# A denser pace of expert gathers in the middle groups, and expert choice that may run on into the dense stage

## The chip, the cores and the metric

The kernel runs on one core of one Trainium2 chip. The metric is the device time of one execution in microseconds (us). The engines are named as in the profile: PE (TensorE matmul), PEld (its weight loads), DVE (VectorE), ACT (ScalarE), POOL (GpSimd) and SP (SyncE, which here only issues DMAs).

## The reference, cut to what matters

One layer over 1152 rows of width 1024, taken as nine tiles of 128 rows (tiles 0 to 7 and a sample tile, here row 8). First a mixer (a gated convolution and an RWKV-7 branch with many projections), then PEER, a retrieval over 16384 single-neuron experts:

```python
q = (xt @ wq).reshape(PEER_BLOCK, PEER_HEADS, 2, PEER_HALF)
s = jnp.einsum('thpd,hpnd->thpn', q, keys).astype(jnp.float32)
s_top, i_top = lax.top_k(s, PEER_TOPK)
...
sc, pos = lax.top_k(cand, PEER_TOPK)
eidx = jnp.take_along_axis(cidx, pos, axis=-1)
gate = jax.nn.softmax(sc, axis=-1)
u = jnp.take(U, eidx, axis=0)
act = jax.nn.gelu(jnp.einsum('thkd,td->thk', u, xt).astype(jnp.float32))
coef = (gate * act).astype(xt.dtype)
return jnp.einsum('thk,thkd->td', coef, jnp.take(V, eidx, axis=0))
```

Each token has 8 heads of 16 experts, so a tile of 128 tokens needs 128 gathers from `U` and 128 from `V`, each of 128 rows of 4 KB.

## The kernel before, in words

The mixer runs over three groups of three tiles: `base(0)`, `base(1)`, `base(2)`. Below, these are group 0 and the two middle groups, 1 and 2. Each streams all the weights through `split_w`: a 256 KB load on SP, a copy to `wh` on ACT (line 246) and the subtraction that gives `wl` on POOL (line 248). PE then multiplies. A group ends with the scores of the expert keys and their top 16 on DVE (`top`).

PEER is done in two ways. Rows 3 to 6 (`DENSE`) are done densely: `dense()` multiplies these 512 tokens with all the experts. Its first half, `gates_of`, builds coefficient tables out of one-hot tiles (`o1`, `o2`), and `hidden_ahead` runs beside it. Its second half, here the main loop, runs over 32 groups of four blocks of 128 experts; per group it has 72 matmuls into `ph` and 96 into `po`, and DVE makes 8 `vl`, 8 `acc`, 4 `ge`, 4 `ph` and 3 `ul` tiles. Rows 0, 1, 2, 7 and 8 are done sparsely: `sparse_u` issues 128 gathers from `peer_u` on POOL (line 1026), each followed by a dot product on DVE into `hu` (called a u step here); `sparse_v` issues 128 gathers from `peer_v` (line 1073), each followed by four matmuls into `sv` on PE in the trace (a v step). All gathers share six `gt` buffers. That makes 1280 steps, 640 of each kind. `side()` runs the v steps of one row beside the u steps of the next, two by two, or one kind alone when the other has no row ready.

Two tables of numbers set the order. `run()` lays out the main work and counts its PE time in `P.ns`; it puts in a sparse step whenever `state[1]` falls behind `P.ns`, and then moves `state[1]` on by `pace()`. In the middle groups that is `PACE_B`, its first number while both kinds run and its second while one runs alone. In the dense stage it is the time that is left over the steps that are left, so that the steps end 40 us (`EARLY`) before the counted end. `route()` is the expert choice of one row; it is cut into pieces of `SPREAD` units by `yield`, and `routes()` takes the rows one after the other, with at most three sparse rows between their choice and the end of their `sparse_v` (`live`). `weave` puts the pieces of `routes()` between the pieces of a group; what is left of them when the group is at its end follows in one block. A scheduler then orders the instructions of each engine once more by its own estimate of time, so that the order on an engine isn't quite the order of the code; on the chip each engine keeps to its order.

Of the kernel before, what the change touches and what calls it, by code (L numbers as in the profile page):

```python
# [27 lines left out]
DENSE = [3, 4, 5, 6]  # L28
# [2 lines left out]
NPT = 8  # L31
NSL = 27
LAT = 350
SPREAD = 16
PACE_B = (1400, 1900)
EARLY = 40e3
NGT, NGD = 6, 0
AWAY = [4, 5, 6, 7]
# [58 lines left out]
def body(ctx, tc, A):  # L97
# [13 lines left out]
    def T(pool, shape, dt=F32, tag=None, bufs=None):  # L111
        _c[0] += 1
        kw = {}
        if tag is not None:
            kw["tag"] = tag
        if bufs is not None:
            kw["bufs"] = bufs
        return pool.tile(shape, dt, name=f"{tag or 'c'}_{_c[0]}", **kw)
# [31 lines left out]
    P = Tensor()  # L150

    class Vector:


        last = None
# [26 lines left out]
    def rk_ps(shape=(128, 512)):  # L182
        return T(spare[0], list(shape), F32, spare[1], spare[2])
# [116 lines left out]
    def slot():  # L300
        return T(bp, [128, 392], F32, "sl", NSL)
# [15 lines left out]
    def base(g):  # L317
# [6 lines left out]
        last = g == len(GROUPS) - 1  # L324
# [546 lines left out]
        def top(hp, q):  # L871
            kt_ = T(bp, [128, 128], F32, "keys", 2)
            nc.sync.dma_start(kt_, A["keys"][hp])
            ps = rk_ps()
            for j in range(len(tiles)):
                P.matmul(ps[:, j * 128:(j + 1) * 128], q[:, j * 128:(j + 1) * 128], kt_, start=True, stop=True)
            sc = slot()
            S.activation(sc[:, :n], ps[:, :n], AF.Copy)
            for j in range(len(tiles)):
                s_ = sc[:, j * 128:(j + 1) * 128]  # L880
                va, vb = vals[j][:, hp, 0:8], vals[j][:, hp, 8:16]
                V.max(va, s_)
                V.max_index(idxs[j][:, hp, 0:8], va, s_)
                V.match_replace(out=s_, in_to_replace=va, in_values=s_, imm_value=NEG)
                V.max(vb, s_)
                V.max_index(idxs[j][:, hp, 8:16], vb, s_)

        for hp in range(16):
# [8 lines left out]
            q = slot()  # L897
            S.activation(q[:, :n], ps[:, :n], AF.Copy)
            yield
        def end():  # L900
            top(15, q)
            for j in range(len(tiles)):
                route_q.append((row0 + j, vals[j], idxs[j]))

        if last:
            end()
        else:
            rest.append(end)

    def route(row, vals, idxs):  # L910
# [13 lines left out]
        for h in range(8):  # L924
            V.max(sc[:, h, 0:8], cand[:, h])
            V.max_index(pos[:, h, 0:8], sc[:, h, 0:8], cand[:, h])
            V.match_replace(out=cand[:, h], in_to_replace=sc[:, h, 0:8], in_values=cand[:, h], imm_value=NEG)
            V.max(sc[:, h, 8:16], cand[:, h])
            V.max_index(pos[:, h, 8:16], sc[:, h, 8:16], cand[:, h])
            yield 3 if row == 0 else SPREAD  # L930
        posf = T(sp, [128, 128], BF, "posf", 1)
        V.tensor_copy(posf, pos.rearrange("p h k -> p (h k)"))
        ix = T(sp, [128, 16, 16], BF, "ixf", 1)
# [12 lines left out]
        for q in range(4):  # L946
            ks, hs = slice(32 * q, 32 * q + 32), slice(2 * q, 2 * q + 2)
            pf = posf[:, ks]
            ge = T(sp, [128, 32, 16], BF, "lk", 2)
            V.tensor_tensor(ge, pf[:, :, None].to_broadcast([128, 32, 16]),  # L950
                            stc[:, None, :].to_broadcast([128, 32, 16]), op=OP.is_ge)
            pr = T(sp, [128, 512], F32, "cand", 1).rearrange("p (a b) -> p a b", b=16)
            V.tensor_tensor(pr.rearrange("p (h k) r -> p h k r", h=2), ge.rearrange("p (h k) r -> p h k r", h=2),
                            d1[:, hs, None, :].to_broadcast([128, 2, 16, 16]), op=OP.mult)
            V.tensor_reduce(i12[:, 2, ks], pr, axis=AX.X, op=OP.add)
            yield 3 if row == 0 else SPREAD
        V.tensor_copy(ints[:, 0], i12[:, 2])
        V.tensor_scalar(ints[:, 1], ints[:, 0], 6, None, op0=OP.arith_shift_right)
        V.tensor_copy(i12[:, 0], ints[:, 1])
# [1 line left out]
        for q in range(4):  # L961
            ks, hs = slice(32 * q, 32 * q + 32), slice(2 * q, 2 * q + 2)
            r2 = T(sp, [128, 32], BF, "r2", 1)
            V.tensor_tensor(r2, posf[:, ks], i12[:, 2, ks], op=OP.subtract)
            ge = T(sp, [128, 32, 16], BF, "lk", 2)
            V.tensor_tensor(ge, r2[:, :, None].to_broadcast([128, 32, 16]),
                            iot[:, None, :].to_broadcast([128, 32, 16]), op=OP.is_equal)
            pr = T(sp, [128, 32, 16], BF, "lk", 2)
            V.tensor_tensor(pr.rearrange("p (h k) r -> p h k r", h=2), ge.rearrange("p (h k) r -> p h k r", h=2),
                            i4[:, hs, 1, None, :].to_broadcast([128, 2, 16, 16]), op=OP.mult)  # L970
            V.tensor_reduce(i12[:, 1, ks], pr, axis=AX.X, op=OP.add)
            yield 3 if row == 0 else SPREAD
        yield 6 if row == 0 else 2 * SPREAD
        gate = T(sp, [128, 8, 16], F32, "gate_d", 1) if row in DENSE else T(sp, [128, 8, 16], F32, "gate", 3)
        V.tensor_tensor(gate, sc, sc[:, :, 0:1].to_broadcast([128, 8, 16]), op=OP.subtract)
        S.activation(gate, gate, AF.Exp)
# [4 lines left out]
        if row not in DENSE:  # L981
            V.scalar_tensor_tensor(i12[:, 2], i12[:, 0], 128.0, i12[:, 1], op0=OP.mult, op1=OP.add)
            ei = T(sp, [128, 128], I32, "ei", 3)
            V.tensor_copy(ei, i12[:, 2])
        yield 6 if row == 0 else SPREAD
        ps = rk_ps()
        if row in DENSE:
            for q, src in enumerate((i12[:, 0], i12[:, 1], gate.rearrange("p h k -> p (h k)"))):
# [5 lines left out]
        else:  # L994
# [1 line left out]
            et = T(sp, [128, 128], I32, "et", 3)  # L996
            V.tensor_copy(et, ps[:, 0:128])
            sparse_q.append((row, ei, et, gate))
        yield 6 if row == 0 else 2 * SPREAD

    more = [None, 0]

# [265 lines left out]
    steps, until = [0], [None]  # L1268
    n_steps = 256 * (9 - len(DENSE))

    def pace(alone):
        if until[0] is None:
            return PACE_B[alone]
        return max(until[0] - P.ns, 0) / (n_steps - steps[0] + 8)
# [17 lines left out]
    def routes():  # L1292
        while rest:
            yield 0.01
        while route_q:
            while route_q[0][0] not in DENSE and live[0] == 3:
                at = P.ns
                yield 0.5
                if P.ns == at:
                    return  # L1300
            live[0] += route_q[0][0] not in DENSE
            yield from route(*route_q.pop(0))


    live, lists = [0], set()
    sparse_q, sparse_v_q, route_q = [], [], []
    run(base(0))
    for g in range(1, len(GROUPS)):
        run(weave([routes()], base(g)))
# [3 lines left out]
    spare[:] = [pd, "ph", 2]  # L1313
    P.in_order = False
    run(weave([routes()], dense()))
    for _ in itertools.chain(state[0] or (), side()):
        pass
    assert not route_q and steps[0] == n_steps


# [70 lines left out]
```

## Time and profile before

| | us |
|---|---|
| median of 3 runs (4288.79 to 4294.24) | 4293.37 |
| the profiled execution, its own time | 4300.95 |
| its span from first to last instruction | 4299.2 |
| group 0 (0 to 529.5) | 529.5 |
| group 1 (529.5 to 1222.2) | 692.7 |
| group 2 (1222.2 to 2009.9) | 787.7 |
| from the last matmul of group 2 to the first of the dense stage | 55.2 |
| coefficient tables (2065.1 to 2545) | 479.9 |
| main loop (2545 to 4036.3) | 1491.3 |
| from the last `po` matmul to the end | 262.9 |

A table of stretches gives the busy time of each engine in each of these seven stretches, with the granted clock of TensorE as a share of full speed and the mean share of the 16 DMA engines. A row of a group of instructions gives the busy time of the group, the mean time of one, the idle time of its engine just before them and what ended that. Lists of waits give the total, the number and the longest.

### The profile page before, as it was taken

What the parts mean: (1) busy time and instruction counts of PE and PEld (TensorE: products, weight loads), DVE (VectorE), ACT (ScalarE), POOL (GpSimd) and SP (SyncE); (2) the same over time, 40 slices, a digit from 0 to 9 for tenths busy, and PEclk for the clock granted to TensorE, in tenths of its full rate; (3) what the DMA queues carried; (4) which work ended last, traced back from release to release, by engine and by line L of the source; (5) the groups of instructions that cost most, each with busy time, mean ns of one, the idle gap of its engine ahead of it and who ended that gap; (6) DMA issues with size and microseconds to landing.
All of it is one profiled execution on the core that took longest, in us unless ns stands there. A gap on an engine that the chain in (4) does not pass through costs nothing. (4 is left out here: it accounts for less than half of the span.)

```text
span 4299.2 us, 56205 instructions
## 1 busy us (share of the span) xinstructions
PE 3731.6 (87%) x18870; PEld 2680.9 (62%) x18870; DVE 2776.8 (65%) x6970; ACT 1473.3 (34%) x3379; POOL 2216.9 (52%) x2009
## 2 busy tenths in 40 slices
PE   7999977887888888785699969999999999999765
PEld 6777865666656555563477747766667766676411
DVE  3654698968797865868767756666666666656400
ACT  4454523443423333231467742222222222222100
POOL 4434455647777554765365643354434344434454
PEclk9999987979989989987799989999999999999888
DMA  3223445557877665786598787899988899987788
GB/s 96 72 65 101 152 141 180 184 162 239 290 262 255 203 209 195 255 281 228 177 355 325 293 314 272 302 332 336 317 286 287 303 320 330 332 293 269 273 305 321
DMA packets 415584, 1065.20 MB, mean 248 GB/s; under 512 B 44992, under 2 KB 124992, under 8 KB 413248
## 3 DMA queue, kind: packets, MB, share of 16 engines
q0 software_dynamic: 184464, 671.55, 45.4%
q1 hardware_dynamic: 182880, 271.03, 19.5%
q10 hardware_dynamic: 47952, 119.03, 7.5%
q8 instruction: 150, 2.46, 0.2%
q14 instruction: 138, 1.13, 0.1%
HBM read 1000.55 MB, written 61.28 MB: 247 GB/s over the span
## 5 line engine op out<-in xcount | busy, mean ns | idle before, releaser
L1026 POOL DMA_INDIRECT gt<-peer_u,ei x640 | 758.0, 1184 | 1149.5 <-PE sv L142 706.7
L159 DVE SCALAR_TENSOR_TENSOR gt<-gt,xn 128x1024 f32<-128x1024 f32 x640 | 855.0, 1346 | 199.0 <-DMA gt<-peer_u,ei 176.7
L142 PE MATMUL mm<-xT,wh 128*128 128x384 f32 (+1 forms) x2880 | 890.6, 367 | 17.8 <-ACT wh L246 15.8
L1073 POOL DMA_INDIRECT gt<-peer_v,et x640 | 677.4, 1059 | 384.0 <-issue 118.9
L248 POOL TENSOR_TENSOR wl<-raw,wh 128x512 fp32r<-128x512 f32 x432 | 577.6, 1345 | 368.7 <-ACT wh L246 320.3
L142 PE MATMUL sv<-gt,c 128*32 128x512 f32 x2560 | 653.7, 636 | 108.1 <-DMA gt<-peer_v,et 107.4
L142 PE MATMUL po<-vh,ph 128*128 128x512 f32 x2048 | 656.8, 394 | 0.0
L142 PEld LDWEIGHTS mm<-xT,wh 128*128 128x128 f32 x2880 | 556.4, 198 | 96.6 <-issue 54.8
L142 PE MATMUL mm<-xT,wl 128*128 128x384 f32 (+1 forms) x1440 | 509.8, 354 | 56.2 <-POOL wl L248 56.2
L142 PEld LDWEIGHTS po<-vh,ph 128*128 128x128 f32 x2048 | 382.3, 188 | 131.9 <-issue 45.3
L142 PEld LDWEIGHTS sv<-gt,c 128*32 128x32 f32 x2560 | 127.8, 114 | 478.6 <-issue 314.7
L142 PE MATMUL ph<-xth,uh 128*128 128x512 f32 x1024 | 408.4, 399 | 18.3 <-ACT ge L1166 17.4
L246 ACT ACTIVATE wh<-raw 128x512 fp32r<-128x512 f32 x432 | 270.2, 629 | 419.6 <-PE mm L142 217.9
L142 PE MATMUL ph<-xth,ul 128*128 128x512 f32 x1024 | 407.0, 397 | 0.0
L142 PE MATMUL ph<-xtl,uh 128*128 128x512 f32 x1024 | 404.0, 395 | 0.0
L142 PE MATMUL po<-vl,ph 128*128 128x512 f32 x1024 | 402.9, 394 | 0.0
L142 PEld LDWEIGHTS mm<-xT,wl 128*128 128x128 f32 x1440 | 286.6, 199 | 78.2 <-POOL wl L248 70.2
L1193 ACT ACTIVATE vh<-vr 128x512 fp32r<-128x512 f32 x256 | 159.7, 627 | 418.9 <-PE po L142 363.4
L1166 ACT ACTIVATE ge<-ph 128x512 f32<-128x512 f32 x128 | 76.7, 599 | 567.5 <-PE ph L142 567.3
L159 DVE TENSOR_TENSOR ge<-ge,cc 128x512 f32<-128x512 f32 x128 | 88.2, 692 | 257.8 <-ACT ge L1166 244.4
L142 PEld LDWEIGHTS ph<-xth,uh 128*128 128x128 f32 x1024 | 193.4, 189 | 77.4 <-ACT ge L1166 18.9
L159 DVE TENSOR_TENSOR acc<-po,acc 128x512 f32<-128x512 f32 x256 | 168.9, 686 | 106.8 <-PE po L142 106.7
(243 smaller groups left out, 5543.0 us busy)
## 6 DMA issues: line engine op xcount, KB each, us to landing
ur<-u_t SPq DMA_DIRECT2D x128, 512.0 KB, 5.4
vr<-peer_v ACTq DMA_DIRECT2D x256, 256.0 KB, 6.1
raw<-w_in SPq DMA_DIRECT2D x240, 256.0 KB, 3.0
c<-ct ACTq DMA_DIRECT2D x16, 2048.0 KB, 10.1
cc<-c SPq DMA_DIRECT2D x32, 1024.0 KB, 17.3
raw<-peer_wq SPq DMA_DIRECT2D x96, 256.0 KB, 3.9
raw<-w_pab SPq DMA_DIRECT2D x48, 256.0 KB, 3.0
raw<-w_o SPq DMA_DIRECT2D x48, 256.0 KB, 3.4
```

The source lines that it names most:

```text
L142: ins = nc.tensor.matmul(out, lhsT, rhs, **kw)
L159: self.last = getattr(nc.vector, name)(*a, **kw)
L246: S.activation(h, part, AF.Copy)
L248: G.tensor_tensor(lo, part, f32(h), op=OP.subtract)
L1026: G.indirect_dma_start(out=ug, out_offset=None, in_=A["peer_u"], in_offset=bass.IndirectOffsetOnAxis(ap=ei[:, k:k + 1], axis=0))
L1073: G.indirect_dma_start(out=vg, out_offset=None, in_=A["peer_v"], in_offset=bass.IndirectOffsetOnAxis(ap=et[:, t:t + 1], axis=0))
L1166: S.activation(g, ps, AF.Gelu_apprx_tanh)
L1193: S.activation(h, raw, AF.Copy)
```

## The change

`PACE_B` goes from (1400, 1900) to (900, 1500). `SPREAD` becomes a pair: 16 as before in the groups, 8 once the dense stage has begun. `routes()` may stop in the middle of a row at the end of a group and go on from there in the next stage; what is under way is kept in `under`. The last group's rows are chosen in the order 7, 6, 8 in place of 6, 7, 8.

```diff
-SPREAD = 16
-PACE_B = (1400, 1900)
+SPREAD = (16, 8)
+PACE_B = (900, 1500)
...
+            if last:
+                route_q.sort(key=lambda q: [7, 6, 8].index(q[0]) if q[0] > 5 else -1)
...
-            yield 3 if row == 0 else SPREAD
+            yield 3 if row == 0 else SPREAD[until[0] is not None]
...
     def routes():
         while rest:
             yield 0.01
-        while route_q:
-            while route_q[0][0] not in DENSE and live[0] == 3:
-                at = P.ns
-                yield 0.5
-                if P.ns == at:
-                    return
-            live[0] += route_q[0][0] not in DENSE
-            yield from route(*route_q.pop(0))
-
-
-    live, lists = [0], set()
+        while route_q or under[0]:
+            if under[0] is None:
+                ns = 0.5
+                if route_q[0][0] in DENSE or live[0] < 3:
+                    live[0] += route_q[0][0] not in DENSE
+                    under[0] = route(*route_q.pop(0))
+            if under[0]:
+                ns = next(under[0], None)
+                if ns is None:
+                    under[0] = None
+                    continue
+            at = P.ns
+            yield ns
+            if P.ns == at:
+
+                return
+
+
+    live, lists, under = [0], set(), [None]
```

What this does to the order of the engines is shown at three places. In the rows, a name is a tile with a number of its own.

PE at the end of the program before, from the last rows of the dense main loop (`po`) on; `sv_28786` is row 7's v sum, `sv_32947` row 8's:

```order
L142 MATMUL po_35481<-vl_35540,ph_35314 128x512
L142 MATMUL po_35481<-vh_35538,ph_35316 128x512
L142 MATMUL sv_28786<-gt_32720,c_108 32x512
L142 MATMUL sv_28786<-gt_32714,c_108 32x512
L142 MATMUL sv_28786<-gt_32720,c_108 32x512
L142 MATMUL sv_28786<-gt_32714,c_108 32x512
```

PE in the changed program where the last `sv` rows stand (`sv_32381` is again row 8's):

```order
L142 MATMUL sv_32381<-gt_35045,c_108 32x512
L142 MATMUL sv_32381<-gt_35001,c_108 32x512
L142 MATMUL po_35105<-vh_35127,ph_34550 128x512
L142 MATMUL po_35106<-vh_35127,ph_34548 128x512
L142 MATMUL po_35106<-vl_35129,ph_34548 128x512
L142 MATMUL po_35106<-vh_35127,ph_34550 128x512
```

Before, 272 `sv` rows (136 v steps, two rows each) stand behind the last `po`; now none does, and some 240 rows of `ph` and `po` follow the last `sv`.

PE before, from the end of group 2 to the first matmul of the dense stage (`po` from `xr`); `rk` from `i` and `gate_d` are the transposes at the end of the expert choice of rows 5, 6 and 7:

```order
L142 MATMUL rk_18573<-keys_18571,sl_18549 128x128 x3
L147 MATMUL rk_18603<-c_74,i_3971_17463 128x128 x2
L147 MATMUL rk_18603<-c_74,gate_d_18596 128x128
L142 MATMUL sv_17632<-gt_18410,c_108 32x512
L142 MATMUL sv_17632<-gt_18404,c_108 32x512
L142 MATMUL sv_17632<-gt_18410,c_108 32x512
L142 MATMUL sv_17632<-gt_18404,c_108 32x512
L147 MATMUL rk_18729<-c_74,i_4214_18668 128x128 x2
L147 MATMUL rk_18729<-c_74,gate_d_18722 128x128
L147 MATMUL rk_18858<-c_74,i_4246_18794 128x128
L147 MATMUL po_18877<-c_74,xr_18875 128x128 x4
```

PE in the changed program at the same place:

```order
L142 MATMUL mm_19291<-xT_17974,wh_19300 128x384
L142 MATMUL rk_19373<-keys_19371,sl_19351 128x128 x3
L142 MATMUL sv_14321<-gt_17763,c_108 32x512
L142 MATMUL sv_14321<-gt_17756,c_108 32x512
L142 MATMUL sv_14321<-gt_17763,c_108 32x512
L142 MATMUL sv_14321<-gt_17756,c_108 32x512
L142 MATMUL sv_14321<-gt_17820,c_108 32x512
L142 MATMUL sv_14321<-gt_17814,c_108 32x512
L142 MATMUL sv_14321<-gt_17820,c_108 32x512
L142 MATMUL sv_14321<-gt_17814,c_108 32x512
L147 MATMUL po_19418<-c_74,xr_19416 128x128 x4
```

The transposes of the expert choice no longer stand ahead of the first dense matmul; on DVE their work is spread between the one-hot tiles of the first three quarters of `gates_of`.

DVE in the main loop before (`gt` with `hu` is the dot product of a u step):

```order
L159 TENSOR_TENSOR acc_23806<-po_27709,acc_23806 128x512
L159 TENSOR_TENSOR vl_27933<-vr_27929,vh_27931 128x512
L159 TENSOR_TENSOR acc_23806<-po_27710,acc_23806 128x512
L159 TENSOR_TENSOR acc_23806<-po_27711,acc_23806 128x512
L159 TENSOR_TENSOR acc_23806<-po_27712,acc_23806 128x512
L159 TENSOR_TENSOR vl_27951<-vr_27947,vh_27949 128x512
L159 SCALAR_TENSOR_TENSOR gt_26474,hu_24593<-gt_26474,xn_24588 128x1024
L159 SCALAR_TENSOR_TENSOR gt_26477,hu_24593<-gt_26477,xn_24588 128x1024
```

DVE in the changed program's main loop, in the fifth of its 32 groups:

```order
L159 SCALAR_TENSOR_TENSOR gt_25539,hu_24299<-gt_25539,xn_24294 128x1024
L159 TENSOR_TENSOR ul_26564<-ur_26560,uh_26562 128x1024
L159 SCALAR_TENSOR_TENSOR gt_25542,hu_24299<-gt_25542,xn_24294 128x1024
L159 SCALAR_TENSOR_TENSOR gt_25545,hu_24299<-gt_25545,xn_24294 128x1024
L159 SCALAR_TENSOR_TENSOR gt_25548,hu_24299<-gt_25548,xn_24294 128x1024
L159 TENSOR_TENSOR ge_26420<-ge_26420,cc_26274 128x512
L159 TENSOR_TENSOR ul_26712<-ur_26708,uh_26710 128x1024
```

In eight of the 32 groups the dots are now about 16 per group with no `sv` beside them, where it was 6 to 12 with 12 to 24 `sv` rows in every group; the last eight groups have no dots at all.

Counted by stage in the two programs, this is where the steps stand:

| steps | before: u, v | changed: u, v |
|---|---|---|
| gathers on POOL by the end of group 1 | 150, 24 | 174, 46 |
| gathers on POOL ahead of the first one-hot tile | 277, 150 | 344, 218 |
| v on PE: ahead of the dense stage / tables / main loop / behind it | 146 / 78 / 280 / 136 | 214 / 150 / 276 / 0 |
| dots on DVE: ahead of the dense stage / tables / main loop and behind it | 275 / 80 / 285 | 342 / 42 / 256 |

## Rows read from the trace of the kernel before

**Rows 1.** The page's first part: busy time, share of the span and instructions
```profile
PE 3731.6 (87%) x18870; PEld 2680.9 (62%) x18870; DVE 2776.8 (65%) x6970; ACT 1473.3 (34%) x3379; POOL 2216.9 (52%) x2009
```

**Rows 2.** Seven stretches: start:end, length, then the columns that the first line names
```profile
core 0: us, PE busy (x) PEld busy (x) DVE busy (x) ACT busy (x) POOL busy (x), PEclk, DMA share, GB/s
0.00:529.50 529.50, 476.25 (x2978) 412.09 (x2979) 277.55 (x963) 261.98 (x690) 229.93 (x225) 0.94 0.32 98
529.50:1222.20 692.70, 550.06 (x3070) 443.91 (x3069) 582.18 (x1626) 256.77 (x679) 442.09 (x366) 0.87 0.63 203
1222.20:2009.90 787.70, 642.91 (x3642) 457.40 (x3639) 580.70 (x1743) 252.97 (x658) 504.44 (x430) 0.90 0.72 239
2009.90:2065.10 55.20, 1.58 (x4) 0.66 (x4) 54.56 (x254) 5.49 (x14) 1.73 (x2) 0.50 0.15 54
2065.10:2545.00 479.90, 421.18 (x2256) 307.19 (x2256) 325.14 (x888) 315.96 (x737) 275.53 (x279) 0.94 0.84 310
2545.00:4036.30 1491.30, 1487.52 (x6381) 1029.63 (x6383) 932.82 (x1454) 372.08 (x576) 625.20 (x564) 1.00 0.88 304
4036.30:4299.20 262.90, 152.11 (x545) 30.00 (x545) 23.81 (x50) 7.99 (x25) 138.02 (x144) 0.84 0.87 304
```

**Rows 3.** Tile sv: PE instructions, count, ns min/median/max, first and last start
```profile
L142 PE MATMUL sv<-gt,c x2560: 589/592/1064, 1125.1 to 4282.1; 128*32 128x512 f32 x197
L147 PE MATMUL sv<-c,hu x5: 270/273/476, 1120.2 to 4066.2; 128*128 128x128 f32 x5
```

**Rows 4.** Groups behind the last po, 4036.3:4299.2: count | busy, mean ns | idle before
```profile
L142 PE MATMUL sv<-gt,c 128*32 128x512 f32 x544 | 151.7, 694 | 87.2 <-DMA gt<-peer_v,et 86.6 <-DVE c L159 0.6
L1073 POOL DMA_INDIRECT gt<-peer_v,et x132 | 125.6, 951 | 98.6 <-PE sv L142 68.7 <-issue 25.6 <-DVE gt L159 2.5
```

**Rows 5.** Waits of PE between group 2 and the dense stage (2009.9 to 2065.1)
```profile
PE rk L147 <- DVE i L159: 37.4, 2, 24.3
PE rk L147 <- DVE sc L159: 26.5, 1, 26.5
```

**Rows 6.** Groups of instructions in group 1 (529.5 to 1222.2)
```profile
L159 DVE SCALAR_TENSOR_TENSOR gt<-gt,xn 128x1024 f32<-128x1024 f32 x148 | 217.4, 1488 | 8.0 <-DMA gt<-peer_u,ei 5.7 <-PE mm L142 1.2 <-PE sv L142 0.7
L248 POOL TENSOR_TENSOR wl<-raw,wh 128x512 fp32r<-128x512 f32 x142 | 192.4, 1363 | 86.1 <-ACT wh L246 76.5 <-issue 8.1
L1026 POOL DMA_INDIRECT gt<-peer_u,ei x150 | 188.2, 1255 | 117.3 <-DVE gt L159 66.6 <-issue 14.2 <-PE mm L142 5.1
```

**Rows 7.** Groups of instructions in group 2 (1222.2 to 2009.9)
```profile
L159 DVE SCALAR_TENSOR_TENSOR gt<-gt,xn 128x1024 f32<-128x1024 f32 x127 | 195.1, 1544 | 66.3 <-DMA gt<-peer_u,ei 64.2 <-PE mm L142 1.3 <-issue 0.4
L248 POOL TENSOR_TENSOR wl<-raw,wh 128x512 fp32r<-128x512 f32 x144 | 191.5, 1341 | 54.3 <-ACT wh L246 45.5 <-issue 6.2 <-PE sv L147 1.0
L1026 POOL DMA_INDIRECT gt<-peer_u,ei x127 | 144.4, 1137 | 133.9 <-PE sv L142 56.2 <-DVE gt L159 39.1 <-issue 13.7
L1073 POOL DMA_INDIRECT gt<-peer_v,et x127 | 141.3, 1113 | 91.9 <-DVE gt L159 36.2 <-PE sv L142 21.5 <-issue 16.6
```

**Rows 8.** Groups of instructions in the main loop (2545 to 4036.3)
```profile
L142 PE MATMUL sv<-gt,c 128*32 128x512 f32 x1122 | 268.1, 598 | 0.0
L159 DVE SCALAR_TENSOR_TENSOR gt<-gt,xn 128x1024 f32<-128x1024 f32 x283 | 343.3, 1220 | 72.9 <-DMA gt<-peer_u,ei 67.2 <-issue 3.1 <-DMA gt<-peer_v,et 1.9
L159 DVE TENSOR_TENSOR vl<-vr,vh 128x512 fp32r<-128x512 f32 x256 | 174.7, 687 | 50.1 <-ACT vh L1193 50.1
L159 DVE TENSOR_TENSOR acc<-po,acc 128x512 f32<-128x512 f32 x255 | 168.2, 686 | 106.8 <-PE po L142 106.7
L159 DVE TENSOR_TENSOR ul<-ur,uh 128x1024 fp32r<-128x1024 f32 x89 | 109.0, 1225 | 14.6 <-ACT uh L1155 14.0 <-PE po L142 0.3 <-DMA cc<-c 0.3
L159 DVE TENSOR_TENSOR ge<-ge,cc 128x512 f32<-128x512 f32 x128 | 88.2, 692 | 257.8 <-ACT ge L1166 244.4 <-DMA cc<-c 13.3
L159 DVE TENSOR_TENSOR ph<-ge,ph 128x512 fp32r<-128x512 f32 x128 | 87.9, 689 | 49.7 <-ACT ph L1236 48.4 <-issue 0.8 <-PE po L142 0.3
```

**Rows 9.** Groups of instructions of the coefficient tables (2065.1 to 2545)
```profile
L142 PE MATMUL sv<-gt,c 128*32 128x512 f32 x312 | 80.6, 639 | 14.5 <-DMA gt<-peer_v,et 14.5
```

More of the change, by code (lines that the diff above doesn't have):

```diff
@@ L955, in route @@
             V.tensor_reduce(i12[:, 2, ks], pr, axis=AX.X, op=OP.add)
-            yield 3 if row == 0 else SPREAD
+            yield 3 if row == 0 else SPREAD[until[0] is not None]
         V.tensor_copy(ints[:, 0], i12[:, 2])
@@ L971, in route @@
             V.tensor_reduce(i12[:, 1, ks], pr, axis=AX.X, op=OP.add)
-            yield 3 if row == 0 else SPREAD
-        yield 6 if row == 0 else 2 * SPREAD
+            yield 3 if row == 0 else SPREAD[until[0] is not None]
+        yield 6 if row == 0 else 2 * SPREAD[until[0] is not None]
         gate = T(sp, [128, 8, 16], F32, "gate_d", 1) if row in DENSE else T(sp, [128, 8, 16], F32, "gate", 3)
@@ L984, in route @@
             V.tensor_copy(ei, i12[:, 2])
-        yield 6 if row == 0 else SPREAD
+        yield 6 if row == 0 else SPREAD[until[0] is not None]
         ps = rk_ps()
@@ L998, in route @@
             sparse_q.append((row, ei, et, gate))
-        yield 6 if row == 0 else 2 * SPREAD
+        yield 6 if row == 0 else 2 * SPREAD[until[0] is not None]
     more = [None, 0]
@@ L1317, in body @@
         pass
-    assert not route_q and steps[0] == n_steps
+    assert not route_q and not under[0] and steps[0] == n_steps
 def kernel(**inputs):
```

## The prediction

> **What bounds the kernel now.** The page first: PE is busy 87% of the span, DVE 65%, POOL 52% [rows 1]. That average mixes stages with different limits, so the table of stretches comes next [rows 2]. In the main loop PE is busy 1487.5 of 1491.3 us at full clock: PE bounds it, and whatever is put on PE there costs its own time. In the coefficient tables PE is busy 421 of 480. In groups 1 and 2 no engine is full (PE 79% and 82%, DVE 84% and 74%, POOL 64% and 64%, DMA 63% and 72%); they wait on one another in small pieces, and the only measure of what a gather costs there is how much longer they take than group 0, which has no gathers. Two stretches are nearly pure loss. In the 55.2 us ahead of the dense stage PE works 1.6 us and DVE 54.6: PE waits there for the expert choice, 37.4 and 26.5 us by the list of waits [rows 5]. Behind the last `po` lie 262.9 us in which only gathers are left: row 8's v sum begins at 4066.2 and ends at 4282.1 [rows 3], and PE waits 86.6 us for gathers to land [rows 4]. The changed order bears on just these two.
>
> **The change part by part.** The sum is made against the profiled execution (4300.95 us, 7.6 over the median of 4293.37).
>
> *The end.* In the changed order no v step stands behind the last `po`, and the last `sv` has about 240 rows of PE work behind it. So the 262.9 us [rows 2] become the finish of the dense rows alone. Before, from the last `sv` (4282.1) to the end of the span (4299.2) it is 17 us for one row [rows 3]; four rows share most of that, and I take 20, with 16 and 35 as ends. **-243 us** (-228 to -247).
>
> *The gap.* The expert choice of rows 5 (its rest), 6, 7 no longer stands on PE between group 2 and the dense stage. What stays is the top 16 of the last key scores and the first `xr`. I take 10 us of the 55.2 as left: **-45** (-25 to -55). The DVE work itself isn't gone; it goes beside the tables (below).
>
> *Groups 1 and 2.* By the counts of the two programs, 427 gathers stand ahead of the first one-hot tile before and 562 now: 135 more, 67 u and 68 v. Group 1 is 163.2 us longer than group 0 with 174 gathers, group 2 258.2 us longer with 254 [rows 2, 6, 7] (group 1's 24 v gathers are from the counts). That is 0.94 and 1.02 us per gather, expert choice and the sample tile included, and the price doesn't rise much with density. From below, a gather could cost only what PE must do for the v sums: 268.1 us for 1122 matmuls, four to a step, is 0.96 us per v [rows 8], so 68 x 0.96 = 65 us with the u steps hidden. From above, the price is that of a stretch with nothing but gathers: 4066.2 to 4282.1 over 128 is 1.69 us [rows 3], so 228 us. The nearest rows are those of the same groups, so I take 1.05: **+142**.
>
> A dot takes 1488 and 1544 ns in groups 1 and 2, where POOL also splits weights, and 1220 in the main loop, where it doesn't [rows 6 to 8]. The 67 dots that move therefore grow by about 0.3 us, 20 us of DVE, which the price per gather already holds. The Trainium skill (SBUF — State Buffer, section "SBUF: two separate sides") speaks against this move: DVE and GpSimd share a pair of ports, and a DVE operation with two SBUF inputs and a GpSimd operation that reads SBUF shut each other out for a whole instruction. The rows agree that there is such a cost, but at a quarter of a whole split of 1.34 us per dot.
>
> *The coefficient tables.* PE gets 150 v steps there in place of 78. Before, 312 matmuls cost 80.6 us there, 1.03 us a step [rows 9]: 72 x 1.03 = 74. Some could fill the 59 us in which PE idles (then about +45); on the other side DVE gets the expert choice of three rows and a rest, some 75 us going by the 54.6 us of the gap [rows 2] for two rows and a rest, and loses 38 dots at 1.22 = 46. DVE is busy 325 of 480 us there, so it has the room, but its order is fixed and PE may wait behind a piece of it. **+75** (+45 to +105).
>
> *The main loop.* Four v steps fewer, 4 x 0.96: -4. But the steps no longer come in pairs all along: for eight of the 32 groups only u steps are there. A group's PE work without v steps is (1491.3 - 268.1) us over the 6381 - 1122 = 5259 other matmuls of the loop, 0.233 each [rows 2, 8], times 168 = 39.1 us. Its DVE work is 8 x 0.687 + 8 x 0.686 + 3 x 1.225 + 4 x 0.692 + 4 x 0.689 = 20.2, and with 16 dots at 1.22 another 19.5: 39.7 us [rows 8]. So in these eight groups DVE draws level with PE. Before, DVE waited 72.9 us over 283 dots for gathers to land, 0.26 each [rows 8], which PE's length hid; here nothing hides it: 16 x 0.26 = 4.2, so 43.9 - 39.1 = 4.8 us a group, 38 in all. If DVE runs ahead of that in the groups on either side it is less. I take +30 (0 to +70). Behind the u steps the loop is bound by PE as before, and six groups with 18 to 34 v steps each have 54 to 72 us for them, over 2 us a gather against 1.69. **+26** (-4 to +66).
>
> *SPREAD, PACE_B and the order 7, 6, 8* have no cost of their own; they act through the counts. Row 6's list must be there for the fourth table; it ends in the second quarter of the counted time of that stage, ahead of need.
>
> *Sum:* -243 - 45 + 142 + 75 + 26 = **-45 us**, 4256 on the profiled scale, 4293.4 - 45 = **4248** on that of the median.
>
> **The rivals.**
> A, *the u steps are free in the middle groups.* PE idles 142 and 145 us in groups 1 and 2 [rows 2], and if the moved u steps fill only that, the term is 65 to 90 in place of 142, and the time 4293 - 97 to 4293 - 122: about **4185**. Against it: group 1 has 150 u and 24 v gathers and yet costs 0.94 a gather.
> B, *POOL's queue is what breaks, and the kernel is slower.* In group 2 a gather holds POOL for (144.4 + 141.3)/254 = 1.12 us and waits in front of it for (133.9 + 91.9)/254 = 0.89 us for one of six buffers [rows 7], and the splits `wl` that PE needs stand behind it in order. If all 2.01 us went to the path, 135 x 2.01 = 271, the sum would be +84; with the price of 1.69 it is +41, **4334**. It decides from 187 us, 1.39 us a gather. Against it: in these two groups the splits themselves wait 86.1 + 54.3 = 140 us, mostly for ACT [rows 6, 7], so POOL has 140 us to give, and 271 - 140 = 131 is near my term.
> C, *DVE bounds more than those eight groups' margin.* If a dot there waits for its gather as in group 2, 66.3/127 = 0.52 us [rows 7], a group costs 39.7 + 8.3 - 39.1 = 9 us over, 71 in all, and if the tables take their upper end too, the sum is -243 - 45 + 142 + 105 + 67 = +26; with the tables as forecast -4: **about 4290**, no change.
> D, *every moved dot meets a whole split*: 67 x 1.34 = 90 us on top of the forecast in the middle groups, sum +45, **4338**. The page named above would give this if the shutting out were met each time; 0.3 of 1.34 us in the rows speaks against it.
> E, *the change doesn't do what it says*, the last v sum still trailing: PE keeps its order, so v steps can't come behind the last `po`; late gathers could only show as PE waits inside the loop. At 1.69 us a gather against the 54 to 72 us per group worked out above, I give this no chance of its own.
>
> **How the numbers follow.** Chances: forecast 0.56 (about 4215 to 4283), A 0.14, B 0.14, C 0.13, D 0.03. A measurement of this kernel tells about 0.2% (8.6 us) from no change. Faster: 0.56 and 0.14, less a little of the forecast's upper end, 0.69. Same: C and that little, 0.14. Slower: B and D, 0.17. For 8 in 10 the range reaches from A's middle to the lower half of B: 4185 to 4315.
>
> **What would show it.** Right: behind the last `po` some 20 us; the gap under 20 us; groups 1 and 2 together some 140 us longer than 1480 (about 745 and 880), with POOL's gathers at 220 and 340; tables about 555; main loop about 1517, with DVE near 95% in eight groups early in it and PE under 95% there. A is right if groups 1 and 2 grow by under 100; B if they grow by over 187 and the waits of PE for `wl` (or of POOL for buffers) grow most; C if PE waits for DVE in the main loop for over 60 us; D if the mean dot in groups 1 and 2 is over 2 us. The prediction as a whole is wrong if the 135 gathers cost over 1.39 us each.

## The result, and the profile after

The changed kernel takes 4177.74 us (4175.54 to 4182.16), against 4293.81 for the kernel before in the same comparison: a ratio of 0.9727 (0.9705 to 0.9749), 116 us less. That lies below the forecast range of 4185 to 4315; the sign was right, the size was not: -121.4 us on the span of the profiled execution (4299.2 to 4177.8) where the sum said -45.

The table of stretches of the kernel after, cut at the events that [rows 2] was meant to be cut at, has the start and end of a stretch, its length, busy time by engine, the granted clock and the DMA share:

```profile
core 0: us, PE busy (x) PEld busy (x) DVE busy (x) ACT busy (x) POOL busy (x), PEclk, DMA share, GB/s
0.00:527.80 527.80, 473.79 (x2979) 410.07 (x2980) 277.04 (x964) 261.55 (x690) 229.25 (x225) 0.95 0.31 98
527.80:1266.00 738.20, 575.15 (x3165) 447.46 (x3164) 610.49 (x1690) 256.23 (x678) 495.44 (x411) 0.88 0.68 224
1266.00:2092.80 826.80, 690.47 (x3793) 465.60 (x3790) 628.11 (x1706) 250.63 (x656) 596.38 (x510) 0.92 0.82 275
2092.80:2109.50 16.70, 6.44 (x24) 1.73 (x23) 16.70 (x105) 0.98 (x2) 11.85 (x10) 0.74 0.91 323
2109.50:2681.70 572.20, 500.61 (x2553) 322.88 (x2553) 349.14 (x1102) 328.11 (x767) 313.46 (x323) 0.95 0.85 308
2681.70:4166.40 1484.70, 1483.53 (x6362) 1030.13 (x6362) 898.77 (x1400) 372.22 (x582) 600.57 (x529) 1.00 0.85 294
4166.40:4177.80 11.40, 0.03 (x1) 0.00 (x0) 6.34 (x14) 3.15 (x11) 2.13 (x4) 0.62 0.45 184
```

One border of the table ahead of the prediction was wrong. The last projection matmul (`mm`) of group 2 ended at 1988.3, and at 2009.9 no matmul ends. All stretches here are cut at the last `mm` of a group. Cut at 1988.3, the kernel before has these three stretches (the tables here end at the main loop's first matmul, 2548.8):

```profile
1222.20:1988.30 766.10, 636.35 (x3619) 455.40 (x3618) 561.68 (x1623) 250.33 (x654) 492.34 (x419) 0.90 0.72 236
1988.30:2065.10 76.80, 8.15 (x30) 2.65 (x29) 73.58 (x373) 8.14 (x18) 13.82 (x13) 0.57 0.37 127
2065.10:2548.80 483.70, 421.20 (x2257) 307.21 (x2257) 328.94 (x894) 319.04 (x743) 275.53 (x279) 0.94 0.84 309
```

So the gap was 76.8 us and group 2 lasted 766.1. With these borders the account of all the runs is below. Lengths are in us, from the profiled executions; "gathers" are those that start on POOL inside the stretch.

| stretch | before | after | difference | forecast |
|---|---|---|---|---|
| group 0 | 529.5 | 527.8 | -1.8 | 0 |
| group 1 (gathers 174, 219) | 692.7 | 738.2 | +45.6 | +142 with group 2 |
| group 2 (gathers 242, 333) | 766.1 | 826.8 | +60.7 | |
| gap ahead of the dense stage | 76.8 | 16.7 | -60.2 | -45 |
| coefficient tables | 483.7 | 572.2 | +88.6 | +75 |
| main loop | 1487.5 | 1484.7 | -2.8 | +26 |
| behind the last `po` | 262.9 | 11.4 | -251.5 | -243 |
| sum | 4299.2 | 4177.8 | -121.4 | -45 |

Differences are taken before rounding. A stretch of one profile repeats only so far: e6_spread16 and e11_more_dve, described below, change nothing in groups 1 and 2, and these took 1565.1 and 1557.4 us together there, 1565.0 in the changed kernel. The expectations below count 550 gathers ahead of the tables, where the part ahead of the prediction has 562; in the trace 561 start ahead of the dense stage, 552 of them in groups 1 and 2.

The two stretches of loss went as the order said. The waits of PE in the gap, 37.4 and 26.5 us before [rows 5], are these after:

```profile
PE sv L142 <- DMA gt<-peer_v,et: 5.6, 1, 5.6
PE po L147 <- DVE sc L159: 4.1, 1, 4.1
PE rk L142 <- ACT sl L898: 0.6, 1, 0.6
```

No `sv` stands in the last stretch, where 544 matmuls stood [rows 4]. The single operations in groups 1 and 2 cost about what they did [rows 6, 7], here the dots and the splits in group 2:

```profile
L159 DVE SCALAR_TENSOR_TENSOR gt<-gt,xn 128x1024 f32<-128x1024 f32 x165 | 243.9, 1484 | 55.9 <-DMA gt<-peer_u,ei 43.5 <-issue 11.6 <-DMA gt<-peer_v,et 0.3
L248 POOL TENSOR_TENSOR wl<-raw,wh 128x512 fp32r<-128x512 f32 x144 | 188.9, 1319 | 16.4 <-ACT wh L246 13.9 <-issue 0.2
```

The splits waited 45.5 us for ACT before and wait 13.9 now: POOL's queue had room, and the change used a good part of it.

### The profile page after: what moved, and what is told of

It reads as the page before. It is cut to its first block, busy times and chain, and to the rows that moved or that the text cites. A ratio compares the mean times of both kernels' runs of the same rounds, so it can differ in the third digit from the quotient of the medians.

```text
span 4177.8 us, 56096 instructions
## 1 busy us (share of the span) xinstructions
PE 3730.0 (89%) x18870; PEld 2677.9 (64%) x18870; DVE 2786.6 (67%) x6970; ACT 1472.9 (35%) x3383; POOL 2249.1 (54%) x2009
## 4 chain that ended last, share of the span: by engine, by line
PE 51%; POOL 7%; DVE 6%; DMA 5%; issue 5%; ACT 2%; POOLq 0%; DVEq 0%; ACTq 0%; SPq 0%
PE po L142 19%; PE ph L142 16%; PE sv L142 10%; PE mm L142 4%; DMA gt<-peer_v,et 3%; POOL wl L248 3%; POOL gt L1075 2%; PE rk L142 2%; DVE gt L159 2%; POOL gt L1028 2%; DVE sl L159 1%; ACT ct L1147 1%; DMA cc<-c 1%; DMA gt<-peer_u,ei 1%; DVE bc L159 0%
## 5 line engine op out<-in xcount | busy, mean ns | idle before, releaser
L1028 POOL DMA_INDIRECT gt<-peer_u,ei x640 | 803.1, 1255 | 786.8 <-PE sv L142 353.0
L142 PE MATMUL sv<-gt,c 128*32 128x512 f32 x2560 | 651.7, 633 | 76.4 <-DMA gt<-peer_v,et 76.3
L142 PE MATMUL mm<-xT,wl 128*128 128x384 f32 (+1 forms) x1440 | 516.5, 359 | 77.0 <-POOL wl L248 76.8
L159 DVE TENSOR_SCALAR o<-iota,dt 128x128 f32<-128x128 f32 x640 | 180.6, 358 | 125.2 <-PE po L142 125.0
## 6 DMA issues: line engine op xcount, KB each, us to landing
cc<-c SPq DMA_DIRECT2D x32, 1024.0 KB, 13.9
```

Source lines behind the costliest of these rows:

```text
L142: ins = nc.tensor.matmul(out, lhsT, rhs, **kw)
L159: self.last = getattr(nc.vector, name)(*a, **kw)
L1028: G.indirect_dma_start(out=ug, out_offset=None, in_=A["peer_u"], in_offset=bass.IndirectOffsetOnAxis(ap=ei[:, k:k + 1], axis=0))
```

## The experiments

### The two parts apart

The pace alone, put into the kernel before:

```diff
-PACE_B = (1400, 1900)
+PACE_B = (900, 1500)
```

> The kernel before with PACE_B = (900, 1500) alone; routes(), SPREAD and the order of rows as before. By its order no v step stands behind the last po, 256 stand ahead of the first dense matmul, 128 in the tables, 256 in the main loop. Theory 1 (each v step costs its PE time of about 1 us wherever PE is busy and nothing in the gap ahead of the dense stage, and the end of 263 us goes with the pace alone): -251 at the end, +105 in groups 1 and 2, +52 in the tables, -23 in the main loop: about 4175, as fast as the whole change. Rival (the gap is lost time that only the new routes() gives back): about 60 us slower than the whole change, 4238.

Measured: 4255.22 us (4250.52 to 4259.77) against 4299.97, ratio 0.9894 (0.9874 to 0.9915). Theory 1 falls; the rival (4238) is right in kind and still too hopeful. By stretch against before: end -251.5, groups 1 and 2 +46.9 and +56.9, tables +43.6, main loop -31.1, and the gap **+92.4**. The gap's own row:

```profile
2093.70:2263.00 169.30, 78.64 (x199) 13.88 (x198) 134.62 (x480) 6.68 (x17) 104.25 (x91) 0.69 0.86 297
```

Row 0's sum is done within group 2 and all of row 1's v steps now stand ahead of the dense stage, the last 46 of them in the gap itself. So `live` falls, and the old `routes()` no longer stops at row 8: all that is left of rows 5 to 8 comes in one block on DVE (134.6 us busy of 169.3). The v steps meant to fill it stand there too, but PE waits for their gathers:

```profile
PE sv L142 <- DMA gt<-peer_v,et: 84.3, 22, 7.1
PE rk L147 <- DVE i L159: 5.8, 2, 4.9
```

The other part alone, in the changed kernel:

```diff
-PACE_B = (900, 1500)
+PACE_B = (1400, 1900)
```

> The changed kernel with PACE_B = (1400, 1900) as before: the new routes(), SPREAD pair and row order alone. 136 v steps stay behind the last po. Theory 1: the gap ahead of the dense stage falls from 77 to under 20 us, the tables take over the DVE work at some 10 to 20 us, the end stays at 260: about 4245. Rival (the expert choice is on the path in the tables too, so that the gap is given back): 4285 to 4300.

Measured: 4254.44 (4249.05 to 4263.49), ratio 0.9897 (0.9874 to 0.9921). Theory 1 holds nearly, term by term, with a total 9 us too low: gap -56.0 (20.8 us are left), tables +14.4, end -0.8, the rest within 4 us. So each half gives some 45 us alone, and both give 116: the pace takes the end away but makes the gap grow, and the new `routes()` keeps the gap small whatever the pace.

### How dense the middle groups can be

```diff
-PACE_B = (900, 1500)
+PACE_B = (1150, 1700)
```

> The changed kernel with PACE_B = (1150, 1700). 77 gathers more than before ahead of the dense stage, 36 v steps behind the last po. Theory 1 (0.79 us for a gather moved into the middle groups): +61 in groups 1 and 2, -60 in the gap, -6 in the tables, +61 in the main loop, end about 85 (-178): about 4171. Rival (1.05 us a gather as forecast, and the rest as measured): about 4190.

Measured: 4193.61 (4188.25 to 4200.18), ratio 0.9756 (0.9735 to 0.9777). Groups 1 and 2 take +53.0 for 79 gathers (0.67 each), but the 36 v steps behind the last `po` keep 78.6 us there, the main loop gets +66.7 and the tables +13.4 in place of -6. Nearer to the rival's number, but not by its reason: the gather was cheaper than theory 1 had it, the dense stage dearer.

```diff
-PACE_B = (900, 1500)
+PACE_B = (700, 1200)
```

> The changed kernel with PACE_B = (700, 1200). 716 gathers ahead of the first one-hot tile in place of 427 (before) and 550 (the change); 44 v steps in the tables, 256 in the main loop, none behind it. Theory 1 (price in the middle groups stays near 0.8 us a gather: about 1 per v, 0.4 per u): +231 against before in groups 1 and 2, -35 tables, -23 main loop, -251 end, -60 gap: about 4155. Rival (the middle groups saturate; each gather beyond the changed kernel's costs the 1.69 us of a stretch with gathers alone): about 4290.

Measured: 4318.64 (4314.88 to 4326.11), ratio 1.0048 (1.003 to 1.0066), half a per cent slower than before. The rival is right in kind, though 29 us short: group 2 lasts 1043.2 us with 457 gathers where the changed kernel has 826.8 with 333, 216 us for 124 gathers, 1.75 each. Groups 1 and 2 together take 268 us more for 168 gathers, 1.60 each. POOL is busy 69% of group 2, and PE, with 268 gathers for v steps there beside 189 for u steps, waits for them to land (28.0 us in the changed kernel's group 2):

```profile
PE sv L142 <- DMA gt<-peer_v,et: 99.5, 29, 7.5
PE mm L142 <- POOL wl L248: 57.9, 29, 5.4
```

### What a gather costs in the middle groups

The baseline first: the kernel before with almost no step in the middle groups.

```diff
-PACE_B = (1400, 1900)
+PACE_B = (1e9, 1e9)
```

> The kernel before with PACE_B = (1e9, 1e9): all but 6 of the 1280 sparse steps go behind the middle groups. Only the length of groups 1 and 2 is asked for; the rest of the kernel is expected to be longer (more v steps trail). Theory 1 (the forecast's baseline): without gathers groups 1 and 2 last as long as group 0, about 530 us each, and the price of a gather at the old pace is 0.94. Theory 2: the expert choice on DVE, the way groups 1 and 2 are woven and the sample tile make them longer, 560 and 600 us, so that the gathers of the old pace cost only about 0.7 us each.

Measured in one profile (span 4617.5 us, 855.4 of them behind the last `po`):

```profile
0.00:532.60 532.60, 480.05 (x2979) 414.74 (x2980) 277.61 (x964) 261.89 (x690) 229.39 (x225) 0.94 0.31 97
532.60:1081.10 548.50, 484.55 (x2988) 416.04 (x2987) 360.72 (x1332) 254.16 (x677) 231.98 (x200) 0.93 0.30 98
1081.10:1656.80 575.70, 502.68 (x3127) 434.65 (x3125) 367.85 (x1358) 244.60 (x647) 214.11 (x173) 0.90 0.28 87
```

Between the two theories: groups 1 and 2 without gathers last 16 and 43 us longer than group 0, with some 85 us more of DVE busy time each, mostly the expert choice. So the old pace paid (692.7 - 548.5) / 168 = 0.86 and (766.1 - 575.7) / 242 = 0.79 a gather.

Then the parts of the price. Narrower v matmuls in the middle groups of the changed kernel:

```diff
-                    mm = P.matmul(pv[q:q + 32, hf * 512:(hf + 1) * 512], cex[:, lo:lo + 32],
-                                  vgs[c][:, hf * 512:(hf + 1) * 512], start=i == 0, stop=i == 31, side=True)
+                    w = 512 if until[0] is not None or i in (0, 31) else 64
+                    mm = P.matmul(pv[q:q + 32, hf * 512:hf * 512 + w], cex[:, lo:lo + 32],
+                                  vgs[c][:, hf * 512:hf * 512 + w], start=i == 0, stop=i == 31, side=True)
```

> The changed kernel; the matmuls of v steps that are laid out ahead of the dense stage take 64 columns in place of 512, but for the first and the last of each sum (the sums of rows 0 to 2 are left incomplete). All gathers and dots stay. Theory 1 (what a moved gather costs in the middle groups is mostly PE's v work, about 0.96 us a step): groups 1 and 2 together shrink by 140 to 180 us of 1565. Rival (it is POOL's queue and the six buffers): by 40 us or less.

Measured in one profile: groups 1 and 2 do not shrink; they last 749.3 and 837.6, 22 us more in all, with 26 gathers more by the order. Theory 1, PE's own work as the price, falls: 26 gathers at the average price of 0.78 would be 20 of the 22 us. Group 2:

```profile
1280.10:2117.70 837.60, 613.68 (x3835) 498.65 (x3834) 630.99 (x1740) 250.80 (x656) 625.15 (x528) 0.83 0.84 284
```

PE is busy 77 us less than in the changed kernel, and all of it turns into waiting, most of it `mm` for `wl`, here and then in the changed kernel:

```profile
PE mm L142 <- POOL wl L248: 107.6, 45, 6.6
```
```profile
PE mm L142 <- POOL wl L248: 54.1, 35, 4.8
```

The saving was larger than 77 us, but the mean granted clock was also lower, 0.83 in place of 0.92, and the same matmul took longer, as the next row shows (363 ns a piece in the changed kernel's group 2):

```profile
L142 PE MATMUL mm<-xT,wh 128*128 128x384 f32 x737 | 235.7, 379 | 1.1 <-ACT wh L246 1.1
```

Narrower dots:

```diff
-            behind(V.scalar_tensor_tensor(ug, ug, 1.0, xn, op0=OP.mult, op1=OP.mult, accum_out=hu[:, k:k + 1]),
-                   mains[0])
+            w = D if until[0] is not None else 64
+            behind(V.scalar_tensor_tensor(ug[:, :w], ug[:, :w], 1.0, xn[:, :w], op0=OP.mult, op1=OP.mult,
+                                          accum_out=hu[:, k:k + 1]), mains[0])
```

> The changed kernel; the dots of u steps that are laid out ahead of the dense stage take 64 of 1024 columns (the activations of rows 0 to 2 are wrong). All gathers and v sums stay. DVE loses about 340 x 1.3 = 440 us of its 1240 in groups 1 and 2. Theory 1 (a u step costs about 0.4 us there, by DVE): groups 1 and 2 shrink by about 130 us of 1565. Rival (u steps are free, DVE is nowhere on the path): by 30 us or less.

Measured in one profile:

```profile
530.60:1205.10 674.50, 557.19 (x3182) 437.39 (x3181) 438.50 (x1696) 255.70 (x678) 440.18 (x421) 0.91 0.73 252
1205.10:1971.00 765.90, 670.23 (x3787) 455.75 (x3785) 451.41 (x1700) 249.84 (x656) 533.84 (x506) 0.94 0.86 295
```

Groups 1 and 2 shrink by 63.8 and 60.9, 124.6 us for 340 dots, 0.37 each, the size that theory 1 had. Whether it is by DVE isn't shown. DVE loses 349 us of its 1239 there, and POOL, whose own work wasn't touched, is busy 118 us less, mostly because its gathers are issued faster beside the short dots. The gain is close to POOL's 118, so a dot may cost by its own time on DVE or by slowing POOL. Issues of u gathers in group 2 of this kernel and then of the changed kernel:

```profile
L1029 POOL DMA_INDIRECT gt<-peer_u,ei x164 | 161.1, 982 | 135.5 <-PE sv L142 86.5 <-issue 20.4 <-DVE gt L159 10.6
```
```profile
L1028 POOL DMA_INDIRECT gt<-peer_u,ei x168 | 200.4, 1193 | 127.4 <-PE sv L142 77.6 <-issue 29.2 <-DVE gt L159 7.8
```

The Trainium skill (SBUF — State Buffer, section "SBUF: two separate sides") says that DVE and GpSimd share a port pair that one of them holds for a whole instruction. That GpSimd can't write descriptors meanwhile it says of DVE's 2-port modes; of a DVE operation with two SBUF inputs, as the dot is, it says that it contends with a GpSimd instruction that reads SBUF, and infers that writing descriptors isn't held up. The rows show 0.21 us less per issue with short dots. They don't tell what in an issue waits, so neither the port nor another way in which DVE could hold POOL up is shown.

Last, fewer bytes. Here the gathers laid out ahead of the dense stage bring a quarter of a row, from other places of the table, and the engines' work stays:

```diff
-            G.indirect_dma_start(out=ug, out_offset=None, in_=A["peer_u"],
+            w = D if until[0] is not None else 256
+            wideu[k] = w == D
+            G.indirect_dma_start(out=ug[:, :w], out_offset=None,
+                                 in_=A["peer_u"].rearrange("e (q c) -> (e q) c", c=w),
...
+            behind(V.scalar_tensor_tensor(ug, xn, 1.0, xn, op0=OP.mult, op1=OP.mult, accum_out=hu[:, k:k + 1]),
+                   mains[0])
...
+                           vg[:, None, 0:256].to_broadcast([128, 2, 256]))
```

> The changed kernel; each gather that is laid out ahead of the dense stage brings 1 KB a row in place of 4 KB (from a reshaped view, so other data), the v matmuls read these columns twice, and the dots multiply xn with itself into the gathered tile: engine work and waits stay, three quarters of the bytes go. By its order 626 gathers stand ahead of the first one-hot tile in place of 550. Theory 1 (bytes are not on the path; a gather costs its place on POOL and its dot): groups 1 and 2 last 1565 + 76 x 0.8 to 1.0, about 1630 to 1640 us. Rival (landing and the six buffers set the price): 1500 us or less in spite of 76 gathers more.

Measured in one profile:

```profile
528.80:1293.60 764.80, 591.07 (x3222) 449.73 (x3221) 632.86 (x1715) 257.24 (x680) 535.12 (x437) 0.87 0.35 109
1293.60:2182.90 889.30, 715.44 (x3896) 465.59 (x3894) 649.51 (x1767) 251.41 (x655) 674.12 (x562) 0.91 0.38 117
```

That is 89 us more than in the changed kernel, with 78 more gathers in the two stretches (245 and 385), 1.14 each, a little over theory 1's upper end, while the DMA engines are busy half as much. The rival falls. A small saving by the bytes isn't excluded, since at the 1.60 us of e5_pace_denser's extra gathers 78 would cost 125 us.

So of the 0.78 us that a moved gather cost on average, the runs show the dots' part (0.37 a u step, by DVE or by POOL); less work on PE and fewer bytes showed no saving. The rest fits a gather's place in POOL's order, over 1 us of issue each with the splits behind it. No run took POOL's issue away, though, so that is argued and left open.

### DVE in the groups with u steps alone

One more DVE operation ahead of each dot in the dense stage:

```diff
         def dot(k, ug):
+            if until[0] is not None:
+                V.tensor_tensor(ug[:, 0:512], ug[:, 0:512], half[:, 39:40].to_broadcast([128, 512]), op=OP.mult)
```

> The changed kernel with one more DVE operation over 512 columns (it scales part of the gathered row, so the output is changed) ahead of every dot in the dense stage. In the groups of the main loop with only u steps (16 a group) that is about 16 x 0.65 = 10 us of DVE more a group. Theory 1 (DVE stands right below PE there: 39.7 against 39.1 us worked out, no cost shown): those eight groups grow from 39.3 to about 48 us each, 70 in all; the groups with both kinds, where DVE is busy 63%, do not grow. Rival (DVE has real room in all groups, 0 in all).

Measured in one profile: the main loop takes 1490.9 us, +6.2, and 8 v steps moved behind it (end 33.0 in place of 11.4). The expected 70 us didn't come, since the scheduler, which knows the operation, spread the dots over more groups, about 12 each. But there is a stretch of nine groups with u steps alone, counted by DVE's `vl` and `acc` tiles:

```profile
2787.80:3159.50 371.70, 364.56 (x1604) 300.24 (x1603) 364.18 (x590) 110.53 (x168) 132.49 (x113) 1.00 0.86 285
```

DVE is busy 98%, and a group takes 41.3 us, more than the 39.1 us of PE's own work for one. PE is busy 98% too, since it takes `ph` matmuls of later groups ahead (740 where nine groups have 648), and it waits 7.1 us. So DVE sets the pace of its tiles there, and little of that reaches the main loop. In the changed kernel the same kind of stretch, seven groups, reads

```profile
2798.30:3073.30 275.00, 275.00 (x1215) 227.70 (x1214) 259.48 (x420) 83.25 (x129) 146.66 (x114) 1.00 0.97 342
```

PE is full, a group takes 39.3 us, and DVE is busy 37.1 of them. DVE did stand right below PE; it did not hold it up.

### The small parts, and faster versions

The next three share one comparison (before: 4298.86 us).

```diff
-SPREAD = (16, 8)
+SPREAD = (16, 16)
```

> The changed kernel with SPREAD = (16, 16): the expert choice goes on beside the tables in coarser spacing, as in the groups. By the counts of v steps the order hardly moves (148 in the tables, 278 in the main loop). Theory (SPREAD has no cost of its own): within 0.2% of the change, 4170 to 4186. Rival (late lists of rows 7 and 6 hold up the dense stage or the next gathers): 20 us or more slower.

Measured: 4177.7 (4174.18 to 4182.92), ratio 0.9707 (0.9688 to 0.9726): no effect, as expected.

```diff
-                route_q.sort(key=lambda q: [7, 6, 8].index(q[0]) if q[0] > 5 else -1)
+                route_q.sort(key=lambda q: [6, 7, 8].index(q[0]) if q[0] > 5 else -1)
```

> The changed kernel with the last rows chosen in the order 6, 7, 8. Theory (the order has no cost of its own, 144 v steps in the tables, 280 in the main loop): within 0.2% of the change. Rival (row 7's list comes later, u steps start later and v steps trail at the end): 20 us or more slower.

Measured: 4163.28 (4160.8 to 4166.52), ratio 0.9676 (0.9657 to 0.9696). Neither: it is 14 us faster than the kernel with SPREAD 16 beside it, with ranges that don't meet. By stretch against the changed kernel: tables -16.4, group 2 -8.9, main loop +8.1. Six v steps fewer stand in the tables and four more in the main loop; at 1.03 and 0.96 us a step that explains less than half of it. Group 2's part is hardly more than e11_more_dve's -7.9, where nothing in that group was changed.

```diff
-PACE_B = (900, 1500)
+PACE_B = (1050, 1650)
```

> The changed kernel with PACE_B = (1050, 1650): by its order still no v step behind the last po, but 525 gathers ahead of the dense stage in place of 550, 82 v steps in the tables in place of 150, 354 in the main loop in place of 276. Theory (stage prices as measured): -22 in groups 1 and 2, -65 in the tables, +79 in the main loop: about 4170, a little faster than the change. Rival: the v steps that come late wait for gathers and trail, 4185 or more.

Measured: 4170.87 (4170.74 to 4172.8), ratio 0.9694 (0.9675 to 0.9713), with groups 1 and 2 -23.7, tables -70.1, main loop +83.6: the theory, term by term.

Both edits together:

> The changed kernel with PACE_B = (1050, 1650) and the row order 6, 7, 8. No v step behind the last po, 525 gathers ahead of the dense stage. Theory (the two gains of e7 and e8, 14 and 7 us, come from different stages): 4150 to 4165, the fastest so far. Rival (they are the same gain, of fewer v steps in the tables): 4163 to 4171.

Measured: 4190.41 (4179.81 to 4204.88) against 4300.55, ratio 0.9743 (0.9719 to 0.9766). Both expectations miss: it is slower than either edit alone. Its tables take 520.5 us where the pace alone gives 502.2, with the same number of v steps but for two. So the gain of the row order doesn't carry over, and what it was in e7 stays open. The fastest complete version run is the changed kernel with the order 6, 7, 8.

## Why the prediction was wrong, point by point

The step that failed is the price of a moved gather in groups 1 and 2: 1.05 us was taken and 0.78 measured, 36 us of the 76 that the sum was off, because the length without gathers was read from another stage. Next, with 29 us, comes a wait of DVE for gathers in the main loop that was carried over and did not occur.

**The reading of the bounds** was right. The two stretches of loss went, and PE bounds the main loop before and after.

**The end** was forecast at -243 and measured -251.5. Four rows finish in 11.4 us, not 20: three of ACT's eight passes over them (`ph` from `acc`) begin before the last `po` ends, and the rows overlap.

**The gap** was forecast at -45 from 55.2 us; it was -60.2 from 76.8. What is left, 16.7, is within what was taken; the start was misread, and the error moved 21.6 us of the gap into group 2. With the border as it was read then, the gap is -38.5 and groups 1 and 2 grow by 84.6, so that their miss is larger still.

**Groups 1 and 2** are the term that was mis-sized most: +142 forecast, +106.3 measured, for 136 gathers by the trace, 0.78 each and not 1.05. Two steps made it too large. Group 0 stood in for groups 1 and 2 without gathers, and e3_no_middle shows those 16 and 43 us longer; with their own baseline the old pace reads 0.86 and 0.79. The prediction said that the expert choice and the sample tile were in its price, and still charged them to gathers that bring neither. Then a margin for density was put on top. The price of a further gather was 0.67 to e4_pace_between's density, 0.94 from there to the changed kernel's (53 us for 57 gathers) and 1.60 from there to e5_pace_denser's. A stretch repeats to some 8 us, so a rise between the first two isn't sure; the last is. 0.8 x 136 would have given 109.

**The coefficient tables:** +75 forecast, +88.6 measured. Both parts had been worked out, 74 for 72 v steps and some DVE work that may come to the path; e2_routes_only measures the second alone at +14.4, and 74 + 14.4 = 88.4. Taking only the first was the error. The same sum meets e8_pace_1050 (18.5, measured +18.4), but e7_order678 took 10 us less and e13_both 16 us more than it gives, so how close it comes here is in part luck.

**The main loop:** +26 forecast, -2.8 measured; the four v steps fewer are -4. The +30 for the groups with u steps alone did not come. DVE did come near PE, but both parts of its 43.9 us a group were too large. The 4.2 us of waits for gathers, which were nearly all of the 4.8 that went over PE's length, did not occur: the dots in the row below have 0.0 us of idle time before them. POOL had the gathers there ahead of need and itself waited 115.2 us for dots to free a buffer:

```profile
L1028 POOL DMA_INDIRECT gt<-peer_u,ei x112 | 145.8, 1302 | 127.1 <-DVE gt L159 115.2 <-issue 10.1 <-DVE acc L159 0.9
```

And DVE's work of 39.7 us was added up from mean durations, which overlap: in the trace an instruction mostly begins some 0.08 us before the end of the one ahead of it. In the stretch of seven groups shown above the groups of DVE rows add up to

```profile
L159 DVE SCALAR_TENSOR_TENSOR gt<-gt,xn 128x1024 f32<-128x1024 f32 x113 | 135.2, 1217 | 0.0
L159 DVE TENSOR_TENSOR vl<-vr,vh 128x512 fp32r<-128x512 f32 x56 | 38.0, 684 | 1.1 <-ACT vh L1195 1.1
L159 DVE TENSOR_TENSOR acc<-po,acc 128x512 f32<-128x512 f32 x57 | 37.3, 684 | 9.7 <-PE po L142 9.7
L159 DVE TENSOR_TENSOR ul<-ur,uh 128x1024 fp32r<-128x1024 f32 x22 | 26.8, 1219 | 1.2 <-ACT uh L1157 1.2
L159 DVE TENSOR_TENSOR ge<-ge,cc 128x512 f32<-128x512 f32 x30 | 20.6, 689 | 1.9 <-ACT ge L1168 1.9
L159 DVE TENSOR_TENSOR ph<-ge,ph 128x512 fp32r<-128x512 f32 x29 | 19.9, 685 | 1.6 <-ACT ph L1238 1.6
L159 DVE DVE_READ_ACCUMULATOR gt<-gt,xn 128x1 f32 x113 | 9.0, 80 | 0.0
```

286.8 us, where DVE is busy 259.5, 37.1 a group. That is below PE's 39.1, with no wait to add. The signs given, DVE near 95% and PE under 95% in these groups, came half true: DVE 94%, PE 100%.

**The misses** are -36 in the middle groups, -29 in the main loop, -15 in the gap, -8.5 at the end, -1.8 in group 0 and +13.6 in the tables, -76.4 in all before rounding. All but the tables went the same way. In the gap and the groups part of that is the misread border.

**Two smaller slips** changed no term. The 0.89 us that POOL waits ahead of a gather in rival B isn't all for a buffer: by [rows 7] what PE's `sv` and DVE's `gt` ended is 153 us, 0.60 a gather. And 39.1 us with 18 v steps at 0.96 is 56 us, not 54.

**The rivals.** A was nearest in number (4185), and its sign came true at the borders then used (groups 1 and 2 grew by 84.6, under 100; by 106.3 at the right ones). Its mechanism isn't borne out: it had the u steps free and the v steps paid at PE's price, where short dots save 0.37 us a u step (e10_narrow_dots) and narrow v matmuls save nothing in all (e9_narrow_sv, with the clock lower). B's point exists, but further out: between 552 gathers, which cost 0.78, and 720 (e5_pace_denser), where the kernel is slower than before; and there PE waits for gathers to land more than for splits. C falls: PE waits for no DVE instruction in the main loop; even with more DVE work (e11_more_dve) the loop grew by only 6.2 us. D falls: a dot takes 1446 and 1484 ns in groups 1 and 2, no more than before. E falls: no v step trails. What the prediction didn't see at all is that the pace and the new `routes()` need each other: the pace alone would have made the gap 169.3 us.

## What to carry to other kernels

Take the baseline for "what does this extra work cost in that stage" from the same stage without it, by an experiment if need be, and look for the density at which the price jumps: here a gather cost 0.67 to 0.94 us up to 333 in a group and 1.75 beyond. Add up an engine's work in a stretch from its busy time, not from mean durations, wherever two engines come within a tenth of each other. Two edits that each look small can remove each other's cost: a faster feed brought a serial block to one place, and only letting that block run on made the feed worth its time.

## What the runs showed of the hardware that was not expected

With the v matmuls cut (e9_narrow_sv), group 2 didn't get shorter, and the work that was left took longer: PE was busy 73% of it in place of 84%, the mean granted clock was 0.83 of full speed in place of 0.92, and the main matmuls took 379 ns in place of 363. That is one profile against one. A gather's issue on POOL depends on what DVE does beside it: 1193 ns beside full dots, 982 beside short ones (e10_narrow_dots). Gathers of a quarter of the bytes, with the DMA engines busy 0.38 of group 2 in place of 0.82, did not make groups 1 and 2 shorter, though 78 more gathers stand there (e12_small_gathers).
